# First norm's weight applied to transposed tokens, products per weight tile in the first stage, and GpSimd's clearing moved behind a later block

## The chip, the core and the metric

One core of one Trainium2 chip runs the whole kernel. The metric is the device time of one execution in microseconds (us); 1097.85 us is the median of three runs of the kernel before.

## The reference

Two blocks of a small model on 256 tokens of 1024 features, in float32. The first block is a gated feed-forward stage (1024 to 2816 and back), a mixer with two kinds of attention, and a second feed-forward stage. The second block is a mixer (a recurrence and an attention), a feed-forward stage, another mixer (a state-space recurrence and an attention), and a last feed-forward stage. Every stage starts with a normalisation:

```python
def _rmsnorm(x, g):
    xf = x.astype(jnp.float32)
    r = lax.rsqrt(jnp.mean(xf * xf, axis=-1, keepdims=True) + EPS)
    return (xf * r * g.astype(jnp.float32)).astype(x.dtype)

def _swiglu(x, w_gate, w_up, w_down):
    return (jax.nn.silu(x @ w_gate) * (x @ w_up)) @ w_down
```

The change touches the first normalisation (`ffn1_pre_g`), the products that follow it, and the time at which some tiles of the first mixer are loaded and cleared.

## The kernel before

**Stages.** `run` goes through seven phases: f1 (feed-forward), m1 (mixer), f2, ab (mixer), f3, cd (mixer), f4. Tokens are held as two halves of 128 (h = 0 and 1) in the tile x.

**Two-part products.** A float32 product is made of three products of a shorter float type: high by high, high by low, and low by high. So every operand has a high part (a conversion) and a low part (the difference). For weights this is the class `Stream`: weight tiles of 128 x 1024 come from memory into four raw buffers (`load_to`, line 73, on SyncE's queue), ScalarE converts the high part (`copy_next`, line 89) or VectorE does (line 87), and VectorE, or GpSimd in one place, subtracts for the low part (`sub`, line 94). The load of the tile four places on is issued behind that subtraction. Six high and six low buffers hold tiles ready; `take` hands out tiles and asks for the split of those up to six ahead, and that is where the conversions and subtractions get their place in the engines' queues.

**Order of work.** Nothing reorders instructions: each engine runs its queue in the order in which the program issues to it, and waits by semaphore for operands of other engines. The order in the code is the order on the engine.

**Start of the first stage.** `setup` (line 275 on) loads x and the first four weight tiles, runs five bf16 products on zeros (`WARM`, line 300), loads the row of the first norm's weight on ScalarE's queue and spreads it over the partitions by products with a column of ones (line 304), then issues the loads of the identity and of the table of small constants on GpSimd's queue (lines 307, 311). `ew` (from line 383) squares a half on ScalarE (line 336), lets GpSimd make the reciprocal root (lines 344, 346) and VectorE multiply tokens by root and weight (line 423). `to_t` transposes a half on TensorE (line 370), ScalarE copies the high part out of PSUM (line 373), VectorE makes the low part (line 378). `enter_first` (from line 490) orders these steps by hand for the first stage. `first` (in `ffn`) then makes the 24 products of a half: 128 tokens by 512 columns, gate and up of block 0 side by side, over four weight tiles (line 642), followed by SiLU (line 644) and the multiplication by up (line 645).

**Blocks 1 to 10.** The loop in `ffn` has, for each block j, gate products, up products (`gemm_b2`, lines 535 and 537, with the second taking the low part of the weights), the high part of the result (hh, ScalarE, line 653), its low part (hl, VectorE, line 654), then the hooks of that block, then the down products of the block before (line 523). Each `gemm_b2` and each `down` takes two weight tiles.

**Hooks of f1.** At blocks 2, 4 and 6 one step each of `s5_powers` and `rg_prep` is issued: small tables for later phases. The step at block 4 has ScalarE functions (lines 1240 to 1242). The step at block 6 has a chain of small GpSimd operations (lines 1249 to 1278), a VectorE reciprocal of its result (line 1279), more GpSimd operations (lines 1280 to 1289 and 965), a second VectorE reciprocal (line 966), and GpSimd operations from line 967 on. At block 5 `m1_load` (line 708 on) issues on GpSimd's queue three loads (rope, gqk, maskb) and four memsets of value tiles of the first mixer (line 712). At blocks 8 and 9 GpSimd makes that mixer's tables (line 717).

## Time and profile before

| What | Value |
| --- | --- |
| Median of three runs | 1097.85 us (1097.48 to 1098.08) |
| Profiled execution | 1096.21 us |
| Its span | 1094.4 us, 16125 instructions |
| TensorE busy | 1077.2 us |
| VectorE, ScalarE, GpSimd busy | 738.9, 599.9, 311.6 us |

The profile is of one execution, whose own time is the second line; its span leaves out what lies around the program's instructions. PE is TensorE, PEld its weight loads, DVE VectorE, ACT ScalarE, POOL GpSimd, SP SyncE. A busy share says how long an engine had work, not whether that work was waited for. In a timeline each line gives start, duration, engine, line of the kernel, operation, what is written from what, how many instructions are merged, and in brackets the idle time ahead of it with what ended that. Durations of neighbours overlap, since the engines pipeline, so the time that one more instruction takes is read from start to start.

### The profile page before, as it was taken

The page shows a single profiled execution, that of the slowest core. Times are in us where ns is not written, and L with a number is a line of the kernel's source. Part 1 is how long each engine was busy: PE and PEld are TensorE (multiplying, and loading weights), DVE is VectorE, ACT ScalarE, POOL GpSimd, SP SyncE. Part 2 cuts the span into 40 slices and gives each one's busy share as a digit, 9 for nine tenths or more (in the row PEclk, how much of TensorE's full clock was granted, in tenths as well). Part 3 has the DMA queues.
Part 4 walks back from the last instruction along what each step waited for, and adds up shares of the span by engine and source line. Part 5 has one row for each costly group of instructions (what it writes and reads, how often), then busy time and mean ns, then how long its engine had stood idle before and what let it go on. Part 6 is the DMA issues. An engine that isn't in the chain of part 4 may idle for free.

```text
span 1094.4 us, 16125 instructions
## 1 busy us (share of the span) xinstructions
PE 1077.2 (98%) x5963; PEld 921.1 (84%) x5963; DVE 738.9 (68%) x1021; ACT 599.9 (55%) x956; POOL 311.6 (28%) x562
## 2 busy tenths in 40 slices
PE   9999999999999999999999999999999999999997
PEld 6888888878878888888987888888889888888886
DVE  5666676889576665667765676767778567565564
ACT  5567455656665554556675554554553465554553
POOL 4006840114310000004021699999406100000000
PEclk9999999999999999999999999999999999999999
DMA  8764665661056656646613665565554345656651
GB/s 264 255 199 160 214 204 172 194 213 59 20 190 210 203 173 201 207 167 194 222 47 127 205 198 174 174 201 178 170 174 160 99 135 199 204 174 201 203 170 61
DMA packets 130256, 190.83 MB, mean 174 GB/s; under 512 B 6017, under 2 KB 101249, under 8 KB 130178
## 3 DMA queue, kind: packets, MB, share of 16 engines
q1 hardware_dynamic: 129440, 187.72, 52.7%
q0 software_dynamic: 736, 2.08, 0.8%
q8 instruction: 47, 0.77, 0.3%
q14 instruction: 31, 0.25, 0.1%
q10 hardware_dynamic: 2, 0.00, 0.0%
HBM read 188.73 MB, written 1.05 MB: 173 GB/s over the span
## 4 chain that ended last, share of the span: by engine, by line
PE 88%; DVE 5%; ACT 2%; issue 2%; POOL 1%; DMA 1%; SPq 0%; POOLq 0%; DVEq 0%; ACTq 0%
PE gb L535 27%; PE f L523 21%; PE gb L537 13%; PE gb L523 5%; PE wo L523 5%; PE fh L642 4%; PE gh L523 3%; PE ga L523 2%; DVE wl L94 1%; PE tp L370 1%; PE lg L523 1%; PE o L888 1%; PE M L1390 1%; DMA wraw<-in_w_qkv_dram 1%; ACT wh L89 1%
## 5 line engine op out<-in xcount | busy, mean ns | idle before, releaser
L94 DVE TENSOR_TENSOR wl<-wraw,wh 128x1024 fp32r<-128x1024 f32 x340 | 413.8, 1257 | 105.8 <-ACT wh L89 104.9
L535 PE MATMUL gb<-xt,wh 128*128 128x512 f32 x1280 | 439.1, 390 | 0.0
L89 ACT CAST wh<-wraw 128x1024 fp32r<-128x1024 f32 x341 | 345.3, 1047 | 49.9 <-PE f L523 11.7
L537 PE MATMUL gb<-xt,wl 128*128 128x256 f32 x1280 | 353.9, 277 | 0.0
L535 PEld LDWEIGHTS gb<-xt,wh 128*128 128x128 f32 x1280 | 240.3, 188 | 50.6
L537 PEld LDWEIGHTS gb<-xt,wl 128*128 128x128 f32 x1280 | 240.4, 188 | 1.7
L523 PE MATMUL f<-wh,hh 128*128 128x512 f32 x348 | 138.2, 397 | 0.0
L523 PE MATMUL f<-wh,hl 128*128 128x512 f32 x348 | 137.1, 394 | 0.0
L523 PE MATMUL f<-wl,hh 128*128 128x512 f32 x348 | 136.9, 393 | 0.0
L659 ACT COPY sg<-gb 128x256 f32<-128x256 f32 x80 | 29.9, 374 | 142.2 <-PE gb L537 138.8
L660 DVE TENSOR_TENSOR sg<-gb,sg 128x256 f32<-128x256 f32 x80 | 33.3, 422 | 92.1 <-ACT sg L659 92.1
L344 POOL TENSOR_TENSOR v<-ss 128x1 f32<-128x1 f32 x22 | 6.5, 297 | 293.4 <-ACT xs L336 180.7
L523 PEld LDWEIGHTS f<-wh,hl 128*128 128x128 f32 x348 | 65.3, 188 | 16.9 <-DVE hl L654 0.9
L523 PEld LDWEIGHTS f<-wh,hh 128*128 128x128 f32 x348 | 65.4, 188 | 14.6
L523 PEld LDWEIGHTS f<-wl,hh 128*128 128x128 f32 x348 | 65.4, 188 | 13.3
L523 PE MATMUL gb<-xt,wh 128*128 128x256 f32 x384 | 69.4, 283 | 0.0
L339 POOL TENSOR_SCALAR ss<-ss 128x1 f32<-128x1 f32 x6 | 2.4, 399 | 234.3 <-ACT xs L336 234.3
L659 ACT COPY su<-gb 128x256 f32<-128x256 f32 x80 | 29.2, 366 | 67.2 <-PE gb L537 67.2
L523 PEld LDWEIGHTS gb<-xt,wh 128*128 128x128 f32 x384 | 59.4, 188 | 0.3
L523 PE MATMUL gb<-xt,wl 128*128 128x256 f32 x192 | 54.2, 282 | 0.0
L523 PE MATMUL wo<-wh,xt 128*128 128x512 f32 x160 | 52.4, 399 | 0.0
L653 ACT CAST hh<-sg 128x512 fp32r<-128x512 f32 x40 | 24.8, 621 | 50.1 <-DVE sg L680 50.1
(404 smaller groups left out, 1591.4 us busy)
## 6 DMA issues: line engine op xcount, KB each, us to landing
wraw<-in_ffn_w_down_dram SPq DMA_DIRECT2D x88, 512.0 KB, 3.8
wraw<-in_ffn_w_gate_dram SPq DMA_DIRECT2D x80, 512.0 KB, 3.8
wraw<-in_ffn_w_up_dram SPq DMA_DIRECT2D x80, 512.0 KB, 5.8
wraw<-in_ab_w_in_dram SPq DMA_DIRECT2D x20, 512.0 KB, 4.6
wraw<-in_w_qkv_dram SPq DMA_DIRECT2D x18, 512.0 KB, 3.7
wraw<-in_w_first_dram SPq DMA_DIRECT2D x16, 512.0 KB, 4.3
wraw<-in_cd_w_in_dram SPq DMA_DIRECT2D x16, 512.0 KB, 4.2
wraw<-in_w_out_dram SPq DMA_DIRECT2D x8, 512.0 KB, 3.6
```

Of the source, the lines that this page charges most:

```text
L89: self.nc.scalar.copy(out=h, in_=r)
L94: eng.tensor_tensor(out=l, in0=r, in1=h.bitcast(F32), op=ALU.subtract)
L370: nc.tensor.transpose(p[:, j * P:(j + 1) * P], src[:, (b + j) * P:(b + j + 1) * P], self.ident)
L523: self.nc.tensor.matmul(out=out, lhsT=l, rhs=r, start=start and i == 0, stop=stop and i == n - 1)
L535: self.nc.tensor.matmul(out=p, lhsT=wh[:, k % 4, c], rhs=self.x2[:, k, :], start=k == 0, stop=False, skip_group_check=True)
L537: self.nc.tensor.matmul(out=p[:, S:2 * S], lhsT=wl[:, k % 4, c], rhs=self.xh[:, k, :], start=False, stop=k == 7, skip_group_check=True)
L642: nc.tensor.matmul(out=p, lhsT=l, rhs=r, start=n == 0, stop=n == 23)
L653: nc.scalar.copy(out=hh, in_=t)
L659: nc.scalar.copy(out=t[:, c, :], in_=p[:, 1, :])
L660: tt(out=t[:, c, :], in0=p[:, 0, :], in1=t[:, c, :], op=ALU.add)
L888: nc.tensor.matmul(out=o, lhsT=v, rhs=p, start=i % 2 == 0 and n == 0, stop=i % 2 == 1 and n == 5)
L1390: nc.tensor.matmul(out=pv[:, a, :], lhsT=l, rhs=F[:, a, 0:4, :].rearrange("p s q -> p (s q)"), start=r == 0, stop=r == 1)
```

## The change

The first norm's weight is no longer multiplied on VectorE before the transposes. It comes as eight columns (`g1`) in the table of small constants, and `to_t` applies it while copying out of PSUM: eight ScalarE copies of 128 x 128 with a per-partition scale, and eight VectorE operations for the low part, for each half. The products that spread the weight over the partitions go. The warm products become 15 in setup and 4 more behind the first half's transposes. The identity and the table of small constants are loaded on ScalarE's queue. In `enter_first` the 48 products of block 0 are issued in groups of two, one group for each weight tile, half and kind (0 high by high, 1 high by low weights, 2 low tokens by high weights); the first tile's high part is made by VectorE, no subtraction is on GpSimd, and the weight tiles 4 and 5 are split behind the first half's SiLU. `m1_load` starts with a GpSimd copy of one element for each partition that reads the high part of the current block's result (`self.cur`) and writes into the rope tile. The second load of x is issued ahead of the third weight tile.

```diff
--- before.py
+++ after.py
@@ -33,13 +33,13 @@
 
 NB_RAW = 4
 NB_HL = 6
-WARM = 5
+WARM = (15, 4)
 
 
 SM = {}
 _o = 0
 for _n, _w in (("convw", 16), ("convb", 4), ("ba", 4), ("bx", 4), ("lam", 4), ("glub", 4),
-               ("lr", 16), ("li", 16), ("ldt", 16), ("d", 16)):
+               ("lr", 16), ("li", 16), ("ldt", 16), ("d", 16), ("g1", 8)):
     SM[_n] = (_o, _w)
     _o += _w
 NSM = _o
@@ -105,6 +105,12 @@
     def used(self):
 
         self.free = self.nt
+
+    def early(self, i):
+
+        h, l = self.hl[i]
+        a = self.specs[i][1][0]
+        return h.rearrange("p (a b) -> p a b", a=a), l.rearrange("p (a b) -> p a b", a=a)
 
     def take(self, n, used=True):
         if used:
@@ -283,37 +289,30 @@
                 nc.sync.dma_start(out=self.x[:, h, c], in_=A["x"][128 * h:128 * h + 128, c])
 
         load_x(0)
-        self.ws.load_to(3)
+        self.ws.load_to(2)
         load_x(1)
         self.ws.load_to(NB_RAW)
 
         t = self.g_p.tile([P, D], F32, name="warm", tag="g")
         nc.vector.memset(t[:, 0:256], 0.0)
-        nc.vector.memset(t[:, 256:384], 1.0)
-        warm = t[:, 0:256].bitcast(BF16)
-        g = self.pre_of(0)
-        row = self.g_p.tile([P, D], F32, name="grow", tag="g")
-        i = GAINS.index(g)
-        nc.scalar.dma_start(out=row[0:1, :], in_=A["gains"][i:i + 1, :])
-        p = self.ps("warm")
-        for _ in range(WARM):
-            nc.tensor.matmul(out=p, lhsT=warm[:, 0:P], rhs=warm, start=True, stop=True)
-        self.gains[g] = []
-        for c in (slice(0, 512), slice(512, D)):
-            p = self.ps("grow")
-            nc.tensor.matmul(out=p, lhsT=t[0:1, 256:384], rhs=row[0:1, c], start=True, stop=True)
-            self.gains[g].append(p)
+        self.wz = t[:, 0:256].bitcast(BF16)
+        self.wp = self.ps("warm")
+        self.warm(WARM[0])
         self.ident = self.const.tile([P, P], F32, name="ident")
-        nc.gpsimd.dma_start(out=self.ident, in_=A["c_ident"])
+        nc.scalar.dma_start(out=self.ident, in_=A["c_ident"])
         self.mhalf = self.const.tile([P, 16], F32, name="mhalf")
         nc.gpsimd.memset(self.mhalf, -0.5)
         self.small = self.const.tile([P, NSM], F32, name="small")
-        nc.gpsimd.dma_start(out=self.small, in_=A["smalls"])
+        nc.scalar.dma_start(out=self.small, in_=A["smalls"])
         if self.phases[0] != "f1":
             for _ in self.s5_powers():
                 pass
             for _ in self.rg_prep():
                 pass
+
+    def warm(self, n):
+        for _ in range(n):
+            self.nc.tensor.matmul(out=self.wp, lhsT=self.wz[:, 0:P], rhs=self.wz, start=True, stop=True)
 
     def sv(self, name, i=None, n=1):
         o, w = SM[name]
@@ -359,7 +358,8 @@
         self.nxt += 1
         self.xh, self.xl = (t[:, o:o + 8 * S].rearrange("p (a t) -> p a t", a=8) for o in (oh // 4, ol // 4))
 
-    def to_t(self, h, src, oh, ol, n=8):
+    def to_t(self, h, src, oh, ol, n=8, gain=None):
+
 
         nc = self.nc
         lo = []
@@ -370,12 +370,22 @@
                 nc.tensor.transpose(p[:, j * P:(j + 1) * P], src[:, (b + j) * P:(b + j + 1) * P], self.ident)
             pv = p[:, :m * P].rearrange("p (a t) -> p a t", a=m)
             hv = oh[:, b:b + m, h * P:(h + 1) * P]
-            nc.scalar.copy(out=hv, in_=pv)
-            lo.append((ol[:, b:b + m, h * P:(h + 1) * P], pv, hv))
+            if gain is None:
+                nc.scalar.copy(out=hv, in_=pv)
+                lo.append((ol[:, b:b + m, h * P:(h + 1) * P], pv, hv))
+                continue
+            for j in range(m):
+                g = gain[:, b + j:b + j + 1]
+                nc.scalar.activation(out=hv[:, j, :], in_=pv[:, j, :], func=AF.Copy, scale=g)
+                lo.append((ol[:, b + j, h * P:(h + 1) * P], pv[:, j, :], hv[:, j, :], g))
 
         def low():
-            for o, pv, hv in lo:
-                nc.vector.tensor_sub(out=o, in0=pv, in1=hv.bitcast(F32))
+            for o, pv, hv, *g in lo:
+                if g:
+                    nc.vector.scalar_tensor_tensor(out=o, in0=pv, scalar=g[0], in1=hv.bitcast(F32), op0=ALU.mult,
+                                                   op1=ALU.subtract)
+                else:
+                    nc.vector.tensor_sub(out=o, in0=pv, in1=hv.bitcast(F32))
 
         return low
 
@@ -409,6 +419,13 @@
                 nc.vector.tensor_tensor(out=xv[:, c], in0=a, in1=xv[:, c], op=ALU.add)
         yield
         next(xsq)
+        if not self.fin:
+            r = next(xsq)
+            yield
+            for c in c2:
+                nc.vector.tensor_scalar(out=xs[:, c], in0=xv[:, c], scalar1=r, scalar2=None, op0=ALU.mult)
+            yield xs
+            return
         gs = list(zip(c2, self.gain2(gname)))
         early = accs and not gpost and h == 0
         if early:
@@ -489,27 +506,53 @@
 
     def enter_first(self, e0, e1, first):
 
-        V, G = self.nc.vector, self.nc.gpsimd
+        V, ws = self.nc.vector, self.ws
+        g = self.sv("g1")
         for _ in range(3):
             next(e0)
-        self.ws.copy_next()(G)
         xs = next(e0)
-        self.ws.copy_next(V)(V)
-        next(e1)
-        next(e1)
         self.new_xt()
-        low = self.to_t(0, xs, self.xh, self.xl)
-        split = self.ws.copy_next()
+        low = self.to_t(0, xs, self.xh, self.xl, gain=g)
+        self.warm(WARM[1])
+        lo = ws.copy_next(V)
+        put = first(None, None)
+        put(0, 0, 0)
+        lo(V)
+        put(0, 0, 1)
+        lo = ws.copy_next()
         low()
-        split(V)
-        next(e1)
-        self.ws.copy_next()(V)
+        for _ in range(3):
+            next(e1)
+        put(0, 1, 0)
+        put(0, 0, 2)
+        lo(V)
+        put(0, 1, 2)
+        put(0, 1, 1)
         xs = next(e1)
-        self.ws.ahead = 4
-        first(0, lambda: self.to_t(1, xs, self.xh, self.xl)())
-        self.ws.ahead = NB_HL
-        self.ws.split_to(NB_HL)
-        first(1, None)
+        lo = ws.copy_next()
+        low = self.to_t(1, xs, self.xh, self.xl, gain=g)
+        lo(V)
+        put(0, 2, 0)
+        put(0, 2, 2)
+        lo = ws.copy_next()
+        low()
+        lo(V)
+        for i in range(3):
+            put(1, i, 0)
+        put(0, 2, 1)
+        for i in range(3):
+            put(1, i, 1)
+        put(0, 3, 0)
+        put(1, 3, 0)
+        put(0, 3, 2)
+        for i in range(3):
+            put(1, i, 2)
+        put(0, 3, 1)
+        put(0, None, None)
+        put(1, 3, 2)
+        ws.take(4)
+        put(1, 3, 1)
+        put(1, None, None)
 
 
     def mm3(self, out, prods, start, stop, late=False, mid=None):
@@ -628,7 +671,32 @@
                 hh, hl = hts[c // 2]
                 return hh[:, c % 2, :], hl[:, c % 2, :]
 
+            def shut(h, p):
+                sg = fp.tile([P, S], F32, name="sgf", tag="sgf", bufs=2)
+                nc.scalar.activation(out=sg, in_=p[:, 0:S], func=AF.Silu)
+                tt(out=sg, in0=sg, in1=p[:, S:2 * S], op=ALU.mult)
+                st[h] = sg
+
+            def parts():
+
+                banks, n, w = [self.ps("fh0"), self.ps("fh1")], [0, 0], {}
+
+                def put(h, i, x):
+                    if i is None:
+                        return shut(h, banks[h])
+                    if i not in w:
+                        w[i] = self.ws.early(i)
+                    t = slice(h * P, (h + 1) * P)
+                    for k in range(2):
+                        nc.tensor.matmul(out=banks[h], lhsT=(self.xl if x == 2 else self.xh)[:, 2 * i + k, t],
+                                         rhs=w[i][x == 1][:, k, :], start=n[h] == 0, stop=n[h] == 23)
+                        n[h] += 1
+
+                return put
+
             def first(h, mid):
+                if h is None:
+                    return parts()
                 if h == 0:
                     st["w"] = self.ws.take(4)
                 p = self.ps(f"fh{h}")
@@ -640,10 +708,7 @@
                     if mid and n == 24 - 12 // self.after:
                         mid()
                     nc.tensor.matmul(out=p, lhsT=l, rhs=r, start=n == 0, stop=n == 23)
-                sg = fp.tile([P, S], F32, name="sgf", tag="sgf", bufs=2)
-                nc.scalar.activation(out=sg, in_=p[:, 0:S], func=AF.Silu)
-                tt(out=sg, in0=sg, in1=p[:, S:2 * S], op=ALU.mult)
-                st[h] = sg
+                shut(h, p)
 
             def split(t, j):
                 hh = fp.tile([P, 2, S], F32R, name="hh", tag="hh")
@@ -679,6 +744,7 @@
                 gather(su, self.gemm_b2())
                 tt(out=sg, in0=sg, in1=su, op=ALU.mult)
                 split(sg, j)
+                self.cur = hts[j][0]
                 for f in (hooks or {}).get(j, []):
                     f()
                 if accs is None:
@@ -705,6 +771,8 @@
 
     def m1_load(self):
         nc, A = self.nc, self.A
+
+        nc.gpsimd.tensor_copy(out=self.rope[:, 0, 0, 0:1], in_=self.cur[:, 0, 0:1].bitcast(F32))
         nc.gpsimd.dma_start(out=self.rope, in_=A["c_rope"])
         nc.gpsimd.dma_start(out=self.gqk, in_=A["gqk"].partition_broadcast(P))
         nc.gpsimd.dma_start(out=self.maskb, in_=A["c_maskb"])
@@ -1738,7 +1806,7 @@
         "lam": ch(g["ab_lambda_2"][0]), "glub": ch(g["cd_glu_b_2"][0]),
         "lr": st(g["cd_lam_re_2"][0]), "li": st(g["cd_lam_im_2"][0]),
         "ldt": st(np.repeat(g["cd_log_dt_2"][0][:, None], 64, 1)),
-        "d": np.tile(g["cd_d_2"][0].reshape(16, 32).T, (4, 1)),
+        "g1": g["ffn1_pre_g"].reshape(8, P).T, "d": np.tile(g["cd_d_2"][0].reshape(16, 32).T, (4, 1)),
     }
     A["smalls"] = np.concatenate([parts[n] for n in SM], 1)
     gb = lambda a: a.reshape(16, 2, 64, 16).transpose(1, 2, 0, 3).reshape(P, 16, 16)
```

## Rows read from the trace of the kernel before

**Rows 1.** The page: the span's busy time by engine.
```profile
PE 1077.2 (98%) x5963; PEld 921.1 (84%) x5963; DVE 738.9 (68%) x1021; ACT 599.9 (55%) x956; POOL 311.6 (28%) x562
```
**Rows 2.** The chain that ended last, start of the run: start us, us, what.
```profile
17.43 0.87 PE tp L370 x8
18.30 6.47 PE fh L642 x28
```
**Rows 3.** Timeline of TensorE and its weight loads, first 25 us.
```profile
1.19 2.31 PE L300 MATMUL warm<-warm 128*128 128x512 bf16 x5 [1.19 <-DVE warm L291]
...
2.44 0.15 PEld L300 LDWEIGHTS <-warm 128*128 128x128 bf16 x1 [0.27 <-issue]
...
7.14 2.02 PE L370 MATMUL tp<-ident,xs 128*128 128x128 f32 x8
...
24.84 0.28 PE L537 MATMUL gb<-xt,wl 128*128 128x256 f32 x1
```
**Rows 4.** Timeline of the other engines, first 25 us.
```profile
5.69 0.75 DVE L423 SCALAR_TENSOR_TENSOR xs<-x,r,grow 128x512 f32<-128x512 f32 x1 [4.42 <-POOL r L346]
...
8.30 0.59 ACT L373 CAST xt<-tp 128x512 fp32r<-128x512 f32 x1 [0.34 <-PE tp L370]
...
10.63 0.63 ACT L336 ACTIVATE pt<-x 128x512 f32<-128x512 f32 x1
...
12.20 1.05 ACT L89 CAST wh<-wraw 128x1024 fp32r<-128x1024 f32 x1 [0.23 <-DMA wraw<-in_w_first_dram]
...
12.39 0.56 POOL L346 TENSOR_TENSOR r<-v,mhalf 128x1 f32<-128x1 f32 x1
12.90 0.61 POOL L708 DMA_DIRECT2D rope<-in_c_rope_dram  x1
...
17.05 1.40 POOL L712 MEMSET vbl<- 128x1536 f32 x1
...
19.26 0.39 ACT L644 ACTIVATE sgf<-fh 128x256 f32<-128x256 f32 x1 [0.29 <-PE fh L642]
```
**Rows 5.** Timeline of ScalarE at 542 us: PSUM reads with a per-partition operand.
```profile
542.65 0.48 ACT L1063 ACTIVATE ta<-za,hba 128x256 f32<-128x256 f32 x1
543.02 0.47 ACT L1064 ACTIVATE tx<-zx,hbx 128x256 f32<-128x256 f32 x1
```
**Rows 6.** Groups by form, whole span: count, busy us, mean ns, idle before.
```profile
L784 ACT CAST vah<-ga 128x128 fp32r<-128x128 f32 x2 | 0.5, 268 | 2.6 <-DVE qa L782 2.6
...
L421 DVE TENSOR_SCALAR xs<-xs,r 128x512 f32<-128x512 f32 x6 | 2.6, 484 | 2.2 <-POOL r L346 2.2
```
**Rows 7.** Timeline of GpSimd, 91 to 124 us.
```profile
91.11 0.21 POOL L1249 TENSOR_TENSOR s5n<-s5n 128x16 f32<-128x16 f32 x1 [72.66 <-ACT s5n L1242]
...
112.15 0.22 POOL L1249 TENSOR_TENSOR s5n<-s5n 128x16 f32<-128x16 f32 x1
...
113.70 0.22 POOL L1249 TENSOR_TENSOR s5n<-s5n 128x16 f32<-128x16 f32 x1
...
115.73 1.20 POOL L1251 TENSOR_TENSOR s5n<-s5n 128x16 f32<-128x16 f32 x1
...
119.11 0.22 POOL L1278 TENSOR_TENSOR s5n<-s5n 128x16 f32<-128x16 f32 x1
...
121.83 0.23 POOL L1285 TENSOR_TENSOR s5n<-s5n 128x16 f32<-128x16 f32 x1 [1.12 <-DVE s5n L1279]
...
123.10 0.22 POOL L965 TENSOR_SCALAR z<-e 128x4 f32<-128x4 f32 x1
```
**Rows 8.** Timeline of ScalarE: the high part of block 5's result.
```profile
104.91 0.62 ACT L653 CAST hh<-sg 128x512 fp32r<-128x512 f32 x1 [2.14 <-DVE sg L680]
```
**Rows 9.** Timeline of VectorE, behind block 6.
```profile
121.44 0.25 DVE L1279 RECIPROCAL s5n<-s5n 128x16 f32<-128x16 f32 x1
...
123.45 4.62 DVE L94 TENSOR_TENSOR wl<-wraw,wh 128x1024 fp32r<-128x1024 f32 x4
```
**Rows 10.** Timeline of TensorE: second of block 7's up products.
```profile
129.64 0.28 PE L537 MATMUL gb<-xt,wl 128*128 128x256 f32 x1
```

## The prediction

> **What bounds the kernel now.** Read the page's line of engines first: TensorE is busy for 98% of the span [rows 1]. So a part of the change matters only where TensorE waits or runs slowly, or where it makes TensorE wait anew. The next view is the chain of waits over the start [rows 2]: once the second half's transposes are done, 28 of the first stage's products go by at 6.47 / 28 = 0.231 us each and the gate products of block 1 follow. The timeline of TensorE shows what lies ahead of that [rows 3]: five warm products from 1.19, then the gain's products, then eight transposes in 2.02 us where eight later ones take 0.87: half the pace, 1.2 GHz instead of 2.4. The second product of block 1, the first that needs a low part of new weights, starts at 24.84; that is the mark by which I time the start. The other engines' timelines [rows 4] show that the second half's squares run at 10.63, its root is ready at 12.39 + 0.56 = 12.95, and the last of the four first weight tiles lands at 12.20. Last, I followed GpSimd and VectorE around the place to which the clearing moves, 90 to 124 us [rows 7 to 9]; there the change adds a wait.
>
> **Warm products.** Start to start they take (2.44 - 1.19) / 3 = 0.42 us, since the fifth weight load runs one product ahead [rows 3]. Fifteen end at 1.19 + 15 x 0.42 = 7.5 if the pace stays, and not before the first half's tokens are scaled: root used at 5.69 [rows 4], plus 0.48 for a plain scaling [rows 6], 6.2. I take 7.0 for the first transpose, so nothing is gained on the 7.14 of before, where the gain's products stood ahead of it; bounds 6.2 and 7.5. The four warm products behind the transposes take 0.9 while TensorE waits for the copies anyway. In this trace the transposes ran at 1.2 GHz after gain products with one row of weights [rows 3]; for dense 128-row products no row says when the pace doubles. At full pace four transposes take 0.45, at half 0.9. The Trainium skill ("TensorE: Matmul & The Clock Gate", Part 1) says that the clock is half by default and that sustained activity releases it; by that the transposes run at full pace, by the row at half, and the sum would differ by 0.45. I take full pace, for these products follow each other without a gap, and keep the half in the range.
>
> **First half.** The copy out of PSUM began 0.28 after the fourth transpose (7.14 + 4 x 0.22 = 8.02, copy at 8.30) [rows 4]. So ScalarE starts at 7.0 + 0.45 + 0.3 = 7.75. Two copies become eight scaled ones of 128 x 128. No row shows one. A plain copy of that size is 0.27 [rows 6], and instructions with a per-token operand on 256 columns start 0.37 apart, 0.11 less than their duration [rows 5]. So spacings between 0.16 and 0.37 are possible; I take 0.27, nearest in shape: 2.15 for eight, done at 9.9. The eight low parts on VectorE (bounded by the same spacings, up to 3 us) follow the first tile's conversion and end near 12, before the next step needs VectorE. The first tile no longer goes to GpSimd; the GpSimd subtraction is off the path.
>
> **Second half.** Behind the eight copies ScalarE converts tile 1, 1.05 each [rows 4], to 10.9, then the squares; from them to the root is 12.95 - 10.63 = 2.32, so 13.2. Scaling 0.05 + 0.48, first transposes at 13.75, eight done at 14.65. By then 6 of 24 groups of two products have run. Eighteen groups, 36 products, remain: 36 x 0.231 = 8.3, to 22.95. Nothing they need is later: tile 3 has landed at 12.2 [rows 4] and its low part is ready near 19.
>
> **Into block 1.** Before, tiles 4 and 5 were converted beside the second half's 24 products. Now they stand behind the first half's SiLU, with four products (0.92) left to cover them. First half's end 22.0, SiLU 0.29 later and 0.39 long [rows 4], conversion 1.05, low part 1.2: the second gate product starts near 25.0 against 24.84. The start as a whole costs 0.2 us. Best case (transposes at 6.2, spacing 0.16): 0.75 + 0.9 less, a gain of 1.4; worst (7.5, half pace, spacing 0.37): 1.95 lost, and 3.9 if the products after 13.75 also run at half pace for some four us, as those of before did through the transposes. The identity and the small tables go to ScalarE's queue before its first square; they are needed at 7 and have five us. GpSimd's memsets and three loads leave 12.90 to 18.45 [rows 4], where TensorE waited for none of them.
>
> **The new wait.** In program order the clearing (three DMA issues, four memsets) stands at block 5, ahead of block 6's GpSimd work on the second model's tables. Before, it waited for nothing, so GpSimd was free and ran block 6's chain early: it began at 91.11, after 72.66 us of waiting for block 4's ScalarE values [rows 7]. Now the clearing starts with a copy that reads block 5's high part, ready at 104.91 + 0.62 = 105.53 [rows 8], and the chain is queued behind it on GpSimd. VectorE's reciprocal at 121.44 needs the chain's last result, and VectorE's queue is in order: behind the reciprocal stand the low parts of block 7's up weights, from 123.45 [rows 9]. TensorE first needs these at 129.64 [rows 10]. Before, they were done at 123.45 + 1.2 = 124.65, with 5.0 us to spare.
>
> Now add up. Copy 0.6 (a small GpSimd operation takes 0.22, beside a VectorE subtraction 1.20 [rows 7]): 106.2. Issues and memsets: 17.05 + 1.40 - 12.90 = 5.55 [rows 4]: 111.75. The chain is 66 operations: eight rounds of six at 113.70 - 112.15 = 1.55, and 18 more at about 0.23 [rows 7]: 12.4 + 4.2 = 16.6. Two VectorE subtractions near 116 stretch an operation by 1 us each, two other VectorE operations about 0.35 each: 19.3, so 131.0 instead of 119.33. From there to the end of the last step that VectorE's second reciprocal awaits was 123.32 - 119.33 = 3.99, of it 1.12 waiting for VectorE [rows 7]: 2.87 remain, 133.9. Low part 0.1 later and 1.2 long: 135.2. TensorE stands from 129.6 to 135.2: **5.5 us**. Floor: copy 0.22, no stretching at all, 2.5 for the last steps: 131.8, 2.2 us. Ceiling: copy 1.20 and two more stretches: near 8. VectorE, ScalarE and the weight loads make the delay good in the 5.5 us of block 7's down products, so I count no second stall. The queue of weight loads is held too, since each is issued after a subtraction; it has the same cover. The copy's read also holds the buffer that block 8 writes, three blocks later: free. The tables made from the moved loads are used only in the next phase, and a shift of the start moves both sides of the stall alike.
>
> **Sum.** 0.2 + 5.5 = 5.7. The profiled execution took 1096.21 (span 1094.4, 1.8 around it), 1.64 under the median 1097.85. So its like becomes 1101.9, and the median 1103.5. What a measurement can tell from no change: 0.2%, 2.2 us.
>
> **Rivals.** *Clock falls in the stall (0.28).* TensorE idles 5.5 us; nothing in this trace idles so long at full pace, so no row speaks to it but the half pace at the start. If it falls, four us of products at half pace add 2.0: 1105.5. The skill's page, in its section on HAM oscillation, says that a long idle gap puts the clock back to half; whether this gap does, no run here shows yet. *Slow start (0.07).* The worst start, 3.9, with the stall: 1107.2. *Stall nearly covered (0.12).* GpSimd meets no VectorE subtraction, the stall is at its floor of 2.2 and the start at its best, -1.4: 1098.6, no change that can be told. It decides if the chain ends by 128. *Faster (0.06).* The first stage follows the weights' landing instead of ScalarE's order: tile 3 converted at 12.20 + 1.05 = 13.25, then nine groups, 18 x 0.231 = 4.2, 17.4; then the way into block 1, 2.0, 19.4: 5.4 less. With the stall at its floor: 1094.7. It wins if the start saves over 2.2 us more than the stall costs; against it, ScalarE's queue puts eight copies, a conversion and two squares ahead of the second half's transposes. That the change does not do what it says (the clearing not held back) would leave the start alone, 1098.0; it has the covered case's chance.
>
> **Numbers.** Forecast 1103.5 (0.47). The range 1099.5 to 1107.5 holds the forecast with its stall from 2.5 to 8 and its start from a gain of one us, the fallen clock and the slow start, 0.82 in all, and leaves out the two others. Faster 0.06, same 0.12, slower 0.82.
>
> **What would show it.** Right: GpSimd's chain starting near 112 instead of 91; VectorE's reciprocal about 10 us late; one gap of TensorE of about 5 us at block 7's up products, ended by a low part of weights; block 1's second product still near 25; all later gaps as before. Wrong: no such gap, or the chain running ahead of the clearing; block 1 starting before 22; a second gap in blocks 8 to 10; or products after the gap at half pace, which makes it the first rival.

## The result and the profile after

The kernel after takes 1105.12 us (median of four runs, 1103.99 to 1105.49) against 1097.84 for the kernel before (four runs, 1097.48 to 1098.08): a ratio of 1.0063, interval 1.0051 to 1.0075. It is slower by 7.3 us. The profiled execution of after took 1104.87, span 1103.1. The forecast had the sign and the place, and its 1103.5 came from one gap of TensorE at full clock. What happened is that gap and a fallen clock behind it, the first of the rivals (1105.5). Of all the executions in this study two ran far longer at a lower granted clock (1328.56 us in experiment 5, 1525.31 us of the kernel before beside it), and the ratios leave them out.

The page of after answers to [rows 1]: its line of engines, and one of its groups (what is written from what, count, then busy us and mean ns, then idle time ahead and its releaser).

```profile
PE 1078.1 (98%) x5973; PEld 921.6 (84%) x5973; DVE 735.9 (67%) x1033; ACT 602.3 (55%) x968; POOL 301.8 (27%) x560
...
L580 PE MATMUL gb<-xt,wl 128*128 128x256 f32 x1280 | 355.1, 277 | 6.5 <-DVE wl L94 6.5
```

Busy time hardly moved: 1078.1 against 1077.2. The group L580, which had no idle time before, now has 6.5 us of it, ended by VectorE's low parts of weights. Nearly all of that is one gap. The chain that leads to it starts on GpSimd (its timeline, behind block 5):

```profile
106.25 0.71 POOL L775 COPY rope<-hh 128x1 f32<-128x1 f32 x1 [92.70 <-ACT hh L718]
107.26 0.76 POOL L776 DMA_DIRECT2D rope<-in_c_rope_dram  x1 [0.31 <-POOL rope L775]
...
111.59 1.41 POOL L780 MEMSET vbl<- 128x1536 f32 x1
112.94 0.23 POOL L1317 TENSOR_TENSOR s5n<-s5n 128x16 f32<-128x16 f32 x1
...
116.64 1.27 POOL L1319 TENSOR_TENSOR s5n<-s5n 128x16 f32<-128x16 f32 x1
```

GpSimd stands 92.70 us at the copy, and block 6's chain behind it begins at 112.94 where it began at 91.11 [rows 7]. One operation beside a VectorE subtraction is stretched to 1.27. VectorE's timeline goes on:

```profile
132.12 0.25 DVE L1347 RECIPROCAL s5n<-s5n 128x16 f32<-128x16 f32 x1 [9.58 <-POOL s5n L1346]
134.71 0.18 DVE L1034 RECIPROCAL z<-z 128x4 f32<-128x4 f32 x1 [2.34 <-POOL z L1033]
134.81 4.62 DVE L94 TENSOR_TENSOR wl<-wraw,wh 128x1024 fp32r<-128x1024 f32 x4
```

The reciprocal comes 10.7 us later than in [rows 9], and the four low parts of block 7's up weights follow it in the queue: 134.81 instead of 123.45. TensorE's timeline shows both costs:

```profile
129.62 0.39 PE L578 MATMUL gb<-xt,wh 128*128 128x512 f32 x1
...
129.96 0.39 PE L578 MATMUL gb<-xt,wh 128*128 128x512 f32 x1
136.07 0.58 PE L580 MATMUL gb<-xt,wl 128*128 128x256 f32 x1 [5.72 <-DVE wl L94]
136.45 0.63 PE L578 MATMUL gb<-xt,wh 128*128 128x512 f32 x1
...
137.09 0.63 PE L578 MATMUL gb<-xt,wh 128*128 128x512 f32 x1
...
139.65 0.58 PE L578 MATMUL gb<-xt,wh 128*128 128x512 f32 x1
140.07 0.28 PE L580 MATMUL gb<-xt,wl 128*128 128x256 f32 x1
```

The product that ran at 129.64 in [rows 10] runs at 136.07. A pair of products then takes 0.64 from start to start until 139.65, and 0.34 before the gap: half pace for about 4 us. The table of stretches says the same of the clock (columns: busy us and count, granted clock, DMA share, GB/s):

```profile
129.00:133.00 4.00, 1.35 (x8) 1.00 0.00 0
133.00:134.00 1.00, 0.00 (x0) 0.61 0.00 0
134.00:140.00 6.00, 3.93 (x12) 0.50 0.44 134
140.00:141.00 1.00, 1.00 (x7) 0.97 1.07 346
```

0.61 of full in the stretch from 133 puts the fall, to 1.2 GHz, at about 133.2, in the middle of the gap; the return to 2.4 GHz came near 140.0. So the sum of this execution is 0.41 for the start (second gate product of block 1 at 25.25 instead of 24.84), 136.07 - 129.64 - 0.41 = 6.0 for the gap and 4 / 2 = 2.0 for the half pace: 8.4, of which the prediction's sum had 5.7. (Of the 6.0, 5.72 are idle time by the row; the loop had lost 0.14 before it, and the rest is the overlap that neighbouring products otherwise have.) The spans differ by 8.7. The medians differ by 7.3; the profiled execution of before lay 1.6 under its own median, that of after 0.25.

TensorE's start, to be held against [rows 3]:

```profile
1.19 6.23 PE L315 MATMUL warm<-warm 128*128 128x512 bf16 x15 [1.19 <-DVE warm L297]
7.26 1.04 PE L370 MATMUL tp<-ident,xs 128*128 128x128 f32 x8
...
14.12 1.09 PE L370 MATMUL tp<-ident,xs 128*128 128x128 f32 x8 [0.47 <-DVE xs L426]
```

The first transposes now run at full pace (1.04 for eight, 2.02 before), and still block 1 begins no earlier.

### The profile page after: what moved, and what is told of

It is laid out like the page before. It is cut to its first block, busy times and chain, and to the rows that moved or that the text cites. A ratio compares the mean times of both kernels' runs of the same rounds, so it can differ in the third digit from the quotient of the medians.

```text
span 1103.1 us, 16166 instructions
## 1 busy us (share of the span) xinstructions
PE 1078.1 (98%) x5973; PEld 921.6 (84%) x5973; DVE 735.9 (67%) x1033; ACT 602.3 (55%) x968; POOL 301.8 (27%) x560
## 4 chain that ended last, share of the span: by engine, by line
PE 84%; DVE 6%; ACT 4%; POOL 4%; issue 2%; DMA 0%; POOLq 0%; DVEq 0%; ACTq 0%
PE gb L578 25%; PE f L566 20%; PE gb L580 13%; PE gb L566 5%; PE wo L566 5%; PE fh L710 3%; PE gh L566 3%; DVE wl L94 2%; PE ga L566 2%; PE tp L370 1%; ACT wh L89 1%; PE lg L566 1%; PE o L956 1%; PE fh L691 1%; PE M L1458 1%
## 5 line engine op out<-in xcount | busy, mean ns | idle before, releaser
L580 PE MATMUL gb<-xt,wl 128*128 128x256 f32 x1280 | 355.1, 277 | 6.5 <-DVE wl L94 6.5
L580 PEld LDWEIGHTS gb<-xt,wl 128*128 128x128 f32 x1280 | 241.4, 189 | 8.8 <-DVE wl L94 7.1
L566 PEld LDWEIGHTS f<-wl,hh 128*128 128x128 f32 x348 | 65.4, 188 | 13.2
```

The costliest lines, as they stand in the source:

```text
L566: self.nc.tensor.matmul(out=out, lhsT=l, rhs=r, start=start and i == 0, stop=stop and i == n - 1)
L580: self.nc.tensor.matmul(out=p[:, S:2 * S], lhsT=wl[:, k % 4, c], rhs=self.xh[:, k, :], start=False, stop=k == 7, skip_group_check=True)
```

## The experiments

Ten kernels ran, each beside the kernel before, which took 1097.77 (experiments 1 to 4), 1097.50 (5, 6 and 9) and 1097.15 (7 and 8); each ratio is to the kernel before of its own session. An edit is to the kernel after unless the text names another. The hold is the GpSimd copy of line 775.

**1. Without the hold.** The clearing then runs when GpSimd reaches it, as before the change.

```diff
-        nc.gpsimd.tensor_copy(out=self.rope[:, 0, 0, 0:1], in_=self.cur[:, 0, 0:1].bitcast(F32))
         nc.gpsimd.dma_start(out=self.rope, in_=A["c_rope"])
```

> The changed kernel without the GpSimd copy, so that the clearing waits for nothing again. Theory (the wait is the cause): GpSimd's chain starts near 91 us, VectorE's reciprocal waits for nothing, TensorE has no gap at block 7, and only the start's loss of 0.4 us stays: 1098.3 us. Rival 1 (the new start is the cause): still 1105. Rival 2 (the early clearing collides with the new start): no gap at block 7, but the second gate product of block 1 comes 1 to 2 us after 25.25: 1099.5 to 1100.5.

Measured: 1103.81 (1103.35 to 1105.06), ratio 1.0060 (1.0048 to 1.0073). The gap at block 7 is gone and the time is nearly the same. The loss is elsewhere, at the start. From the timelines of VectorE, GpSimd and TensorE in this run:

```profile
13.14 5.90 DVE L426 TENSOR_SCALAR xs<-x,r 128x512 f32<-128x512 f32 x2 [0.72 <-POOL r L345]
...
17.36 1.39 POOL L779 MEMSET vbl<- 128x1536 f32 x1
...
19.09 1.12 PE L370 MATMUL tp<-ident,xs 128*128 128x128 f32 x4 [4.76 <-DVE xs L426]
...
31.75 0.39 PE L580 MATMUL gb<-xt,wl 128*128 128x256 f32 x1 [0.76 <-DVE wl L94]
```

The second half's scaling takes 5.90 us instead of 0.88 in after: its second instruction, begun at 13.54, alone lasts 5.50, and ends at 19.04, just behind GpSimd's last memset (18.75). TensorE waits 4.76 for it, and its clock falls, as the table of stretches of all engines shows (the granted clock is the third number from the right):

```profile
12.00:20.00 8.00, 2.76 (x14) 1.72 (x12) 7.28 (x4) 2.13 (x6) 6.55 (x9) 0.78 0.62 191
20.00:26.00 6.00, 6.00 (x21) 4.79 (x21) 3.46 (x10) 2.08 (x5) 0.00 (x0) 0.72 0.46 139
```

The clock is at 0.78 in the mean of the first stretch and 0.72 in the second: half from 16.5 to 23.3, of which TensorE works from 19.09 on, so that 4.2 / 2 = 2.1 us are lost. The second gate product comes at 31.75 instead of 25.25. So the hold saves 31.75 - 25.25 = 6.5 us at the new start and costs 8.0 at block 7, and the two kernels differ by 1.3. Before the change the same memsets stood in the same place and cost nothing [rows 4], where VectorE's scaling was another instruction (line 423, token times root times weight, the weight in PSUM): its two began at 15.64 and took 1.40 together, between memsets that went on from 14.58 to 18.45. From the timelines of GpSimd and VectorE in before:

```profile
8.03 2.42 POOL L94 TENSOR_TENSOR wl<-wraw,wh 128x1024 fp32r<-128x1024 f32 x1 [2.37 <-ACT wh L89]
...
14.58 0.65 POOL L712 MEMSET vah<- 128x640 f32 x1
...
8.23 2.77 DVE L87 CAST wh<-wraw 128x1024 fp32r<-128x1024 f32 x1 [0.23 <-DMA wraw<-in_w_first_dram]
...
15.64 1.40 DVE L423 SCALAR_TENSOR_TENSOR xs<-x,r,grow 128x512 f32<-128x512 f32 x2
```

The first and third of these lines show that the trace of before already had a plain VectorE operation that was held by GpSimd: the conversion of a weight tile took 2.77 beside GpSimd's subtraction (2.74 in experiment 2, again beside it), and 0.69 in after, where no subtraction is on GpSimd. No run puts the old scaling into the new start, so that the form of the instruction makes the difference is read from these lines and not tried by itself.

**2. The hold alone, in the kernel before.**

```diff
                 split(sg, j)
+                self.cur = hts[j][0]
...
+        nc.gpsimd.tensor_copy(out=self.rope[:, 0, 0, 0:1], in_=self.cur[:, 0, 0:1].bitcast(F32))
         nc.gpsimd.dma_start(out=self.rope, in_=A["c_rope"])
```

> The kernel before with the GpSimd copy alone. Theory: the gap of about 6 us at block 7's up products and about 2 us of products at half pace behind it, without the start's 0.4: 7 to 8 us more than before, 1105 to 1106. Rival 1 (the new start is the cause): no change, 1097.9.

Measured: 1104.75 (1103.52 to 1105.72), ratio 1.0064 (1.0050 to 1.0077). The timelines of VectorE and TensorE:

```profile
132.19 0.25 DVE L1281 RECIPROCAL s5n<-s5n 128x16 f32<-128x16 f32 x1 [8.84 <-POOL s5n L1280]
...
136.13 0.58 PE L537 MATMUL gb<-xt,wl 128*128 128x256 f32 x1 [5.01 <-DVE wl L94]
136.51 0.63 PE L535 MATMUL gb<-xt,wh 128*128 128x512 f32 x1
```

The one copy put into the kernel before makes the whole loss: the gap, the late reciprocal and the half pace (which lasted here until 141.2, (141.2 - 136.13) / 2 = 2.5 us lost). With the hold in place, the other parts of the change add nothing that shows. The four kernels together: 1097.8 before, 1103.8 with the change without its hold, 1104.8 with the hold alone, 1105.1 with both. Each alone costs 6 to 7 us, and the two do not add up, since the hold keeps the memsets from the new start. This run's second gate product came at 25.94, with the instructions of before (24.84 there): its first weight tile was converted at 8.04 instead of 6.91, after a wait for its load. The mark of the new start lies between 24.67 and 25.65 in the seven runs whose order of the start is that of after (after itself and experiments 3, 4, 5 without the early split, 6, 7 and 8). So the start varies by about 1 us between executions, and after's 0.41 is no loss that can be told.

**3. The clearing at block 4, with its hold.** Its GpSimd work comes a block earlier.

```diff
-                hooks.update({5: [self.m1_load], 8: [lambda: self.m1_tables(0)], 9: [lambda: self.m1_tables(1)]})
+                hooks[4].append(self.m1_load)
+                hooks.update({8: [lambda: self.m1_tables(0)], 9: [lambda: self.m1_tables(1)]})
```

> The changed kernel with the clearing, copy and all, hooked to block 4 instead of 5. The same work stands ahead of GpSimd's chain, but its copy is released by block 4's high part near 88 us, so the chain starts near 95, 4 us late instead of 21. Theory: VectorE waits 2 to 4 us, less than the 5.0 that the low parts had to spare, so TensorE has no gap: 1098.3. Rival 3 (not the wait, but the loads and memsets running beside the loop's work cost the time): still about 1105.

Measured: 1096.84 (1096.35 to 1097.34), ratio 0.9993 (0.9984 to 1.0001). VectorE's timeline:

```profile
123.50 0.25 DVE L1347 RECIPROCAL s5n<-s5n 128x16 f32<-128x16 f32 x1 [1.19 <-POOL s5n L1346]
```

The reciprocal waits 1.19 us and TensorE not at all. Same copy, same clearing, same start: what costs is the place in GpSimd's queue.

**4. The gap filled.** The first of block 7's up products is repeated 24 times ahead of them, each time starting the bank anew, so that TensorE is busy while it would wait.

```diff
+            self.nb2 = getattr(self, "nb2", -1) + 1
+            for _ in range(24 if self.nb2 == 26 else 0):
+                self.nc.tensor.matmul(out=p, lhsT=tiles[0][0][:, 0, c], rhs=self.x2[:, 0, :], start=True, stop=False,
+                                      skip_group_check=True)
```

> The changed kernel with 24 additional products in front of block 7's up products: the first product (high part, k = 0) is repeated into the same bank, each time starting the sum anew, so that the result is the same and TensorE works through most of the gap. Theory (the clock falls because TensorE idles): 24 x 0.231 = 5.5 us fit into the 6.0 us gap, the granted clock stays at full, the first products behind the gap take 0.34 a pair instead of 0.64, and the time falls by about 2.0: 1103.1. Rival 4 (the slow products behind the gap come of something else, as the burst of weight loads at 138 us): the same half pace, 1105.1.

Measured: 1102.86 (1102.45 to 1103.11), ratio 1.0049 (1.0037 to 1.0062). TensorE's timeline in this run:

```profile
130.50 5.76 PE L578 MATMUL gb<-xt,wh 128*128 128x512 f32 x24
136.09 0.39 PE L582 MATMUL gb<-xt,wh 128*128 128x512 f32 x1
...
136.44 0.39 PE L582 MATMUL gb<-xt,wh 128*128 128x512 f32 x1
```

The table of stretches of the same run, with the columns as above:

```profile
133.00:134.00 1.00, 1.00 (x6) 1.00 0.00 0
134.00:140.00 6.00, 6.00 (x33) 1.00 0.49 148
```

Work resumes at 136.09, as late as in after (136.07), and pairs take 0.35 at once, at a clock of 1.00. The median is 2.3 under after's. The intervals of the two ratios overlap, so the trace carries the verdict: where TensorE is kept busy the clock does not fall, and the fall is a term of its own, worth about the 2.0 that the rows give. (The fill lasted to 136.1, some 0.4 longer than the low part needed, which was done near 134.45 + 1.2 = 135.65 in this run; and this run's start was 0.4 later than after's. So the two gaps cannot be compared to the tenth.) The median of 1102.86 lies near the forecast's 1103.5, which was a gap at full clock.

**5. The clearing behind block 6's chain, and the rest of the start's wait.** The first edit puts `m1_load` last of block 6's hooks. The second adds to it one line: the weight tiles 4 and 5 are split as soon as tile 3 has its low part, instead of behind the first half's SiLU.

```diff
-                hooks.update({5: [self.m1_load], 8: [lambda: self.m1_tables(0)], 9: [lambda: self.m1_tables(1)]})
+                hooks[6].append(self.m1_load)
+                hooks.update({8: [lambda: self.m1_tables(0)], 9: [lambda: self.m1_tables(1)]})
```

> The changed kernel with the clearing hooked to block 6, behind the steps that hold GpSimd's chain, so that nothing stands ahead of the chain and nothing of the clearing meets the start. Theory: the chain starts near 91.5 as before, VectorE's reciprocal does not wait, no gap at block 7, the start unchanged at 25.25: within 0.5 us of the kernel with the clearing at block 4, 1096.8, and of before. Rival 5 (the clearing costs time wherever it runs beside the loop): 1099 or more.

```diff
         lo(V)
+        ws.split_to(NB_HL)
         for i in range(3):
```

> The kernel with the clearing behind the chain, and the split of weight tiles 4 and 5 issued right after tile 3's, ahead of the first half's SiLU on ScalarE. Theory: the wait of block 1's first gate products (0.5 us for the high part, 0.8 for the low part, and the half-covered end of the first stage) goes, the second gate product starts near 23.4 instead of 25.25, and the time falls by 1.5 to 1.9 us below the kernel with the clearing behind the chain: about 1095. Rival 6 (tiles 4 and 5 land too late, or the conversions hold up the SiLU, so the start is bound by something else): no change against that kernel.

Measured: the first 1096.77 (1095.85 to 1097.26), ratio 0.9996 (0.9987 to 1.0004); no gap at block 7. With the second, 1094.51 (1094.33 to 1095.03), ratio 0.9974 (0.9965 to 0.9983). TensorE's timeline at the start of block 1, with the clearing behind the chain:

```profile
23.79 0.50 PE L578 MATMUL gb<-xt,wh 128*128 128x512 f32 x1 [0.49 <-ACT wh L89]
25.05 0.39 PE L580 MATMUL gb<-xt,wl 128*128 128x256 f32 x1 [0.76 <-DVE wl L94]
```

The same view with the early split as well:

```profile
22.74 0.39 PE L579 MATMUL gb<-xt,wh 128*128 128x512 f32 x1
22.96 0.28 PE L581 MATMUL gb<-xt,wl 128*128 128x256 f32 x1
```

The split ahead of the SiLU takes both waits away: 25.05 - 22.96 = 2.1, and the medians differ by 2.3. So the new start does win something, and the conversion and the low part behind the SiLU had eaten it. The early split was not tried with the old start.

**6. Half of the clearing behind the chain.** The two large memsets go to a step behind block 6's chain; loads and small memsets stay at block 5 with the hold.

```diff
-        for t in self.va + self.vb:
+        for t in self.va:
             nc.gpsimd.memset(t.bitcast(F32), 0.0)
 
+    def m1_rest(self):
+        for t in self.vb:
+            self.nc.gpsimd.memset(t.bitcast(F32), 0.0)
...
+                hooks[6].append(self.m1_rest)
```

> The changed kernel with the two long memsets of the clearing moved behind block 6's steps; the copy, the loads and the two short memsets stay at block 5. GpSimd's chain then starts 2.7 us earlier, at 110.2. Theory (the delay passes on in full): the gap shrinks from 5.7 to about 3.0 us. If the clock falls only late in a gap (it fell 3.2 us into the gap of the changed kernel), it stays or falls at the very end, and the time is 1097 + 3.0 = 1100; if the clock falls as before, the products behind the gap run at half pace again and it is 1102. Rival 4 (half pace behind the gap comes of something else): half pace in any case.

Measured: 1103.01 (1102.19 to 1103.33), ratio 1.0051 (1.0039 to 1.0063). TensorE's timeline in this run:

```profile
129.64 0.39 PE L578 MATMUL gb<-xt,wh 128*128 128x512 f32 x1
133.74 0.39 PE L580 MATMUL gb<-xt,wl 128*128 128x256 f32 x1 [3.71 <-DVE wl L94]
...
134.31 0.60 PE L578 MATMUL gb<-xt,wh 128*128 128x512 f32 x1
...
137.84 0.28 PE L580 MATMUL gb<-xt,wl 128*128 128x256 f32 x1
```

Its table of stretches:

```profile
133.00:134.00 1.00, 0.26 (x2) 1.00 0.00 0
134.00:140.00 6.00, 6.00 (x27) 0.72 0.79 238
```

Both numbers expected were too low by about a microsecond or more. The chain began 112.94 - 109.80 = 3.1 earlier than in after, the product that waits for the low parts only 136.07 - 133.74 = 2.3, and of both 0.46 is this execution's earlier start (24.79 instead of 25.25): the chain's steps ran into VectorE's subtractions anew (the one at 110.27 took 1.18). And the clock, which had lasted through the gap of 3.7 us, fell 0.6 us after work had begun again; the half pace from 134.3 to 137.8 cost 3.5 / 2 = 1.8, nearly what the longer gap costs. A gap that is a third shorter saves that third and almost nothing of the clock's price.

**7. Few warm products.** The clearing behind the chain (experiment 5), with five warm products and none behind the transposes.

```diff
-WARM = (15, 4)
+WARM = (5, 0)
```

> The kernel with the clearing behind the chain, with 5 warm products in setup and none behind the transposes, as many as before. If the warm products are what brings TensorE to full pace at 7 us, the transposes and the first products run at half pace: the first transposes take 1.8 us instead of 0.9 and ScalarE starts its copies 0.5 us later, the products behind 14 us run at half pace for some us more, and the time rises by 1 to 3 us to 1098 to 1100. Rival 7 (the pace at the start does not depend on them, or what is slow there is covered by other waits): no change.

Measured: 1097.21 (1096.45 to 1098.04), ratio 1.0001 (0.9992 to 1.0010), against 0.9996 with all nineteen. TensorE's timeline:

```profile
6.97 1.97 PE L370 MATMUL tp<-ident,xs 128*128 128x128 f32 x8 [3.47 <-DVE xs L426]
```

The transposes do run at half pace again, and the second gate product came at 25.06 all the same. The warm products buy nothing measurable here, since the first stage's products go on to wait for ScalarE and VectorE; with the early split they were not tried.

**8. Memsets late, loads early.** As experiment 1, without the hold, but with all four memsets in a step behind block 6's chain; only the three loads are issued at the start.

```diff
-        nc.gpsimd.tensor_copy(out=self.rope[:, 0, 0, 0:1], in_=self.cur[:, 0, 0:1].bitcast(F32))
...
+    def m1_rest(self):
         for t in self.va + self.vb:
-            nc.gpsimd.memset(t.bitcast(F32), 0.0)
+            self.nc.gpsimd.memset(t.bitcast(F32), 0.0)
...
+                hooks[6].append(self.m1_rest)
```

> The changed kernel without the copy and with all four memsets behind block 6's steps, so that at the start GpSimd only issues the three loads, from about 13 to 15 us. In the kernel without the copy VectorE's second scaling of the second half lasted until GpSimd's last memset ended. If the memsets hold it, it takes 0.5 us here and the second gate product starts near 25.3; if the issue of loads holds it as well, it ends near 15 and that product starts 1 us later, near 26.3.

Measured: one time, 1096.12, beside 1097.15 for before. GpSimd's and VectorE's timelines:

```profile
12.91 0.76 POOL L775 DMA_DIRECT2D rope<-in_c_rope_dram  x1
...
12.99 0.90 DVE L426 TENSOR_SCALAR xs<-x,r 128x512 f32<-128x512 f32 x2 [0.72 <-POOL r L345]
```

The scaling takes 0.90 while GpSimd issues loads. So it is the memsets that hold VectorE in experiment 1, not the loads.

**9. The second half first.** Experiment 5 with the early split, and x loaded ahead of all weight tiles, both halves squared and scaled before ScalarE converts tile 1, and the groups reordered to suit.

```diff
         load_x(0)
-        self.ws.load_to(2)
         load_x(1)
         self.ws.load_to(NB_RAW)
...
-        for _ in range(3):
-            next(e0)
+        for e in (e0, e1):
+            for _ in range(3):
+                next(e)
...
+        xs = next(e1)
+        l0 = ws.copy_next(V)
+        l1 = ws.copy_next()
+        low1 = self.to_t(1, xs, self.xh, self.xl, gain=g)
```

> The kernel with the clearing behind the chain and a new order of the start: both halves of x are loaded ahead of all weights, the squares of both halves run in the time in which ScalarE waits for the first transposes, the second half's scaling stands ahead of the first tile's conversion, and the products of both halves are taken as weight tiles come; tiles 4 and 5 are split early. Theory (the start is bound by ScalarE's queue: eight copies, a conversion and the squares ahead of the second half's root): the second half's transposes move from 14.1 to about 9, the second gate product to 22, and the time is near 1094. Rival 6 (the start is bound by the landing of the weights or by VectorE): as the kernel with the early split, 1095, or no gain.

Measured: 1093.70 (1093.35 to 1093.87), ratio 0.9968 (0.9956 to 0.9979): the fastest version of the study. TensorE's timeline:

```profile
9.35 1.09 PE L369 MATMUL tp<-ident,xs 128*128 128x128 f32 x8 [0.30 <-DVE xs L425]
10.44 0.71 PE L690 MATMUL fh<-wh,xt 128*128 128x512 f32 x2
...
22.29 0.40 PE L577 MATMUL gb<-xt,wh 128*128 128x512 f32 x1
22.53 0.28 PE L579 MATMUL gb<-xt,wl 128*128 128x256 f32 x1
```

The second half's transposes come at 9.35 instead of 14.12, but the second gate product only 22.96 - 22.53 = 0.4 earlier than with the split alone; the medians differ by 0.8. So ScalarE's queue, which the expectation named as the bound, did hold the second half's transposes, but having them early was worth little. From 10.44 to 22.29 are 11.85 us, of which 48 products at 0.231 [rows 2] fill 11.1: little more is to be had behind the transposes.

## Why the prediction was right, and where it was not

The forecast was right in sign, place and kind, and its range holds the time, but it lies nearer the measured median than its sum deserves. The sum was 5.7 us for the 8.4 that the rows of after show: 2.0 of the missing 2.7 are the clock, 0.5 the gap, 0.2 the start. The median came only 1.6 above the forecast because the forecast added the 1.64 by which before's profiled execution was faster than its median, and after's was only 0.25 faster than its own: that is luck.

- **Warm products and first transposes.** First transpose 7.26 against 7.0, at full pace as taken; the half kept in the range did not come. Experiment 7 shows that the choice did not matter to the time.
- **Eight scaled copies.** ScalarE took 2.18 us for eight, 0.27 apart, as the nearest row had it.
- **Second half.** The root came at 13.55 against 13.2 and the transposes at 14.12 against 13.75; GpSimd's first operation took 0.59, with a VectorE subtraction beside it to 12.86, where the same one took 0.27 before. That is the 0.3 by which block 1 was later than forecast (25.25 against 25.0), within the variation of the start.
- **The new wait.** It was right in place, order and kind. The copy began at 106.25 against 105.53, nearly all of it because ScalarE's high part itself began later (105.56 instead of 104.91), and it was 107.26 - 106.25 = 1.0 to the first issue where 0.6 was taken: 0.71 for the copy and a wait of 0.31 behind it. So the chain began at 112.94 against 111.75, took 132.12 - 112.94 = 19.2 against 19.3, and the low part ended at 134.81 + 1.2 = 136.0 against 135.2. The gap was 6.0 instead of 5.5. No second gap came: the waits of TensorE behind block 7 are those of before, and what follows is shifted by 8.2 to 8.7 to the end.
- **The step that failed: the clock through the stall.** The forecast's sum left it at full because no row of before held so long a gap, and gave the fall a chance of 0.28. The fall came, and cost 2.0 as that rival had it; experiments 2 and 4 show it with the rest of the change away, and gone with the gap filled. The rival's four us of half pace stood in no row that the prediction showed; the runs have 4.0 in after, 5.1 in experiment 2 and 3.5 in experiment 6. The weighing was the fault: the page that the prediction cited for the fall, the Trainium skill's "TensorE: Matmul & The Clock Gate" in its section on HAM oscillation, was, beside the half pace at the start, the only evidence in either direction, and here the trace agrees with it (clock 0.50 from 134 to 140).
- **A premise that failed: the early clearing costs nothing at the start.** The prediction read it from a TensorE that did not wait for GpSimd [rows 4], and priced the change without its hold at 1098.0. That was true of the old scaling. Experiment 1 gives 1103.81, since the plain scaling of the new start is held by the memsets; the conversion that took 2.77 in before was the sign of it. The number of the forecast did not use this, but it hid what the hold does: the memsets have to be kept from the new start (experiments 1 and 8), and only the place in the queue is wrong (experiments 3 and 5). The Trainium skill, "SBUF — State Buffer", in its section on who interferes with whom, says that VectorE's single-source operations such as a scaling can use a pair of ports that GpSimd shares, and that one then waits for the other; the second instruction's 5.50 us in experiment 1, against 0.90 for both in experiment 8, agree with that. What the trace does not explain is the order: by the profile the scaling began at 13.54, before the first memset (14.90), and still lasted until all four were done. The same section says that a VectorE operation with two inputs in SBUF contends only with GpSimd operations that read, and the four subtractions from 107.17 in after, at 1.16 each beside memsets and loads, agree too.
- **The rivals.** Slow start: refuted by the mark at 25.25. Stall nearly covered: refuted by the chain, which ended at 132 and met subtractions. Faster: refuted, and its mechanism was not found in experiment 9 either. It put block 1's mark 5.4 us earlier, near 19.4, with the first stage bound by the landing of the weights; the earliest mark of any run is 22.53, and there TensorE's own products fill 11.1 of the 11.85 us ahead. That experiments 5 and 9 come to 1094.51 and 1093.70, near the rival's 1094.7, is chance: they have no stall at all and a gain of about 2 at the start, where the rival had a stall of 2.2 and a gain of 5.4.

Not tried: the old scaling in the new start; what part of the start's 2.1 us in experiment 5 the conversion has and what part the low part; and how the memsets can hold a scaling that began before the first of them is seen to begin (13.54 and 14.90; the profile's GpSimd spans are rough).

## What to carry to other kernels

A wait put on one queue has the price of everything queued behind it: follow the next work on that engine to its reader, and then what stands behind that reader, until an engine without slack is reached. When a gap of several microseconds opens on TensorE, count the clock's fall as likely: in this kernel all four gaps of 3.7 to 5.7 us brought it (after, experiments 1, 2 and 6), for 1.8 to 2.5 us each on top, whether it came in the gap or just behind it, and in the traces of before and after none of the gaps of up to 1.5 us did. And an instruction that was replaced by a cheaper form must be checked anew against what runs beside it: the old form's freedom from another engine's work need not carry over.

## What the runs showed of the hardware that was not expected

- The clock fell at 134.3 in experiment 6, with TensorE already at work again since 133.74, after an idle time of 3.7 us. It was back at about 137.8. In after the fall came inside the gap (133.2).
- The granted clock in the table of stretches reads 1.00 for the first eight microseconds of after, although its fifteen warm products of 512 columns take 6.23 / 15 = 0.42 each, while four of the same kind behind the first transposes take 1.03 together: half pace and full pace. Here the recorded clock is no reading of the pace until its first change.
- A plain scaling of 128 x 512 on VectorE stood 5.50 us beside GpSimd's memsets where the one ahead of it took 0.49, while loads that GpSimd issued did not hold it (experiment 8). A plain conversion stood 2.77 beside a GpSimd subtraction in before, where others of its form take 0.69.
- A GpSimd copy of one element for each partition took 0.71 and held the next issue back by another 0.31, where a small arithmetic operation on 16 columns takes 0.22.
